# Two MLP products exchanged, two weight splits made earlier, and the last norm's squares and outputs shared out

## The chip, the cores and the metric

The kernel runs on one core of one Trainium2 chip. The time is device microseconds (us) of a whole execution. Before the change the median of three runs is 2811.76 us (2811.71 to 2813.89). Five engines appear: TensorE (PE, matmuls, with the weight loads PEld beside it), VectorE (DVE), ScalarE (ACT), GpSimd (POOL) and SyncE (SP), whose queue issues the DMA transfers in program order.

## The reference

A decoder trunk of two layers over 1024 tokens of width 1024, in float32. Layer 0 mixes tokens by a Conformer convolution, layer 1 by forgetting attention (16 heads); each then reads 256 memory tokens by cross-attention and goes through an MLP; a last RMS norm ends it.

```python
def sqrelu_mlp(h, w1, w2):                       # w1 1024 x 4096, w2 4096 x 1024
    return jnp.square(jax.nn.relu(h @ w1)) @ w2

def conformer_conv(h, ...):                      # ends with
    return u @ w_pw2 + b_pw2

for l in range(2):
    if l == 1:                                   # keys, values, gates of forgetting attention
        hk = rmsnorm(x, kv_norm_g)
        kvf = hk @ kvf_w
        ...
    h = rmsnorm(x, norm_mix_g[l])
    x = x + (conformer_conv(h, ...) if l == 0 else fox_attention(h, fox_wq, fox_wo, k, v, c))
    h = rmsnorm(x, norm_mem_g[l])
    x = x + memory_cross_attention(h, ...)
    h = rmsnorm(x, norm_ff_g[l])
    x = x + sqrelu_mlp(h, ff_w1[l], ff_w2[l])
return rmsnorm(x, final_norm_g)
```

## The kernel before

**Layout.** The residual X lies with features on partitions: 8 chunks of 128 features, each in two halves of 512 tokens, so the unit of work is a 128x512 tile. A float32 product is made of three fast passes: an operand is split into a high part (a rounding copy, on ACT, called high) and a low part (the rest, a subtraction on the DVE, called low; line 148), and high x high, low x high and high x low are added in a PSUM bank. `weights` loads a raw 512 KB weight, optionally multiplies it by a norm's gain (L256, DVE), and splits it (L151 ACT, L148 DVE).

**Stages**, by the profile: convolution layer with the matrices of the memory interleaved (to about 525 us), memory attention (to 713), MLP (713 to 1343), forgetting attention (1343 to 1966), memory attention (to 2157), MLP (2158 to 2793), last norm (to 2809). In the convolution layer and the attentions a scheduler places the instructions, by priorities and by when buffers are free. The MLP's order is written out: within `in_order` each engine takes its instructions in the order of the code.

**The MLP** (`mlp`, from L600) is two matrix products, each done by a recursion with seven products instead of eight (Strassen and Winograd). Work comes in pairs of column groups, g and g+1. A pair has seven products, in the order of `SEVEN`, each for both groups in turn, so a pair is 14 steps. A step is one product of 12 matmuls (4 chunks, 3 passes). `base[g]` is the pair's first step; g below UP = 16 is the up phase, g from 16 is the down phase, and the pair at g = 14 is the turn, with its own order. Each group sums its products in three PSUM banks:

```python
SEVEN = ("a11", "a12", "s2", "s1", "s4", "s3", "a22")
SUM = {"a11": 0, "a12": 0, "s2": 1, "s3": 1, "a22": 1, "s1": 2, "s4": 2}
```

So s2, s3 and a22 go to one bank, s1 and s4 to another, and each product adds to what the bank holds. After each product a row reads the sum as it then stands: in the up phase `rows` (L814) makes the inner activations a11, a12, a21, a22; in the down phase `add_rows` (L967, L971 in the first down pairs) adds it to X. A product may add to a bank once the row of the bank's last product has read it.

What happens at a step is put in lists, `urgent`, `before` and `after`, by `at_once`, `at` and `at_end` with the number of the step. In the up phase the inner a11 and a12 are split at given steps (`split_inner_at`: a high on ACT into a tile `uh`, a step later a low on the DVE into `ul`, both of a pool of four `t` tiles) and both parts stored to DRAM (L845); the sums s1 to s4 of the inner activations are made on POOL (L865) and stored (L826). Raw weights are loaded by `load_raw` (L639) on the same SP queue, and POOL combines them (L647). In the down phase the inner tiles are loaded again (L934, L936) and those stored whole are split there (`high_of_inner`, `low_of_inner`).

**Into forgetting attention.** `start_fox` (L1079) gives the first MLP's last steps the start of the next stage: it loads two raw weights (`wk`, the keys' first chunk, and `fox_wq`, the queries'), normalizes the first half of X chunk by chunk (h, L1095), splits it (L1096 high on ACT, L148 low on the DVE), and among the chunks, in the DVE's order after c = 2 and c = 6, multiplies the raw weights by the gain and splits them. The PE then runs the keys' product for the half, a mean of squares for the second half (L158), the queries' product, and a spread of the second half's factor (L167).

**The second linear of the convolution** (`linear` at the end of `conv_layer`) takes one raw weight per output chunk m = 0 to 7, split beside the products of the chunk before; L324 adds the result to X, once per half.

**The last norm** (from L1422): squares of X (L1006, ACT) are added up (L1014, DVE) as the MLP's last chunks come, a token mean over partitions is a matmul with a column (L158), the power -0.5 is on POOL (L207), and a matmul spreads it over partitions (L167). Eight chunks per half are multiplied by gain and factor (L1428, DVE) and stored.

## Time and profile before

| | |
|---|---|
| median of three runs | 2811.76 us |
| profiled execution, its own time | 2810.81 us |
| its span | 2809.0 us |
| mean granted PE clock | 0.993 |
| PE busy | 2725.0 us (97%) |
| DVE busy | 1991.7 us (71%) |
| ACT busy | 1275.7 us (45%) |
| POOL busy | 720.2 us (26%) |

The profile is one execution. Times count from the span's start. A timeline row gives start, length, engine, line, operation, tiles written and read, and how many instructions were put together; in brackets the idle time ahead and what ended it. A row of the waits gives the total, the number and the longest. A group's row gives, behind the bar, the busy total and the mean of one in ns. A row of windows gives the length, then the busy time (and count) of PE, PEld, DVE, ACT and POOL, the granted clock, the DMA share and GB/s.

### The profile page before, as it was taken

The page shows a single profiled execution, that of the slowest core. Times are in us where ns is not written, and L with a number is a line of the kernel's source. Part 1 is how long each engine was busy: PE and PEld are TensorE (multiplying, and loading weights), DVE is VectorE, ACT ScalarE, POOL GpSimd, SP SyncE. Part 2 cuts the span into 40 slices and gives each one's busy share as a digit, 9 for nine tenths or more (in the row PEclk, how much of TensorE's full clock was granted, in tenths as well). Part 3 has the DMA queues.
Part 4 walks back from the last instruction along what each step waited for, and adds up shares of the span by engine and source line. Part 5 has one row for each costly group of instructions (what it writes and reads, how often), then busy time and mean ns, then how long its engine had stood idle before and what let it go on. Part 6 is the DMA issues. An engine that isn't in the chain of part 4 may idle for free. (4 is left out here: it accounts for less than half of the span.)

```text
span 2809.0 us, 35852 instructions
## 1 busy us (share of the span) xinstructions
PE 2725.0 (97%) x12832; PEld 2247.6 (80%) x12832; DVE 1991.7 (71%) x3119; ACT 1275.7 (45%) x2295; POOL 720.2 (26%) x487
## 2 busy tenths in 40 slices
PE   7999999999999999999899999989999999999998
PEld 6777777888888877888688888878888788878886
DVE  5999984555776577777777777775546855677776
ACT  5112143433465563334466666663424655543332
POOL 0000000000076625784000000000000365625763
PEclk9999999999999999999899999999999999999999
DMA  6334364321265585652123222244213455565651
GB/s 220 120 120 135 110 213 124 102 91 56 80 220 181 188 303 195 214 199 91 61 87 94 89 88 77 86 143 138 96 67 105 144 183 191 203 228 194 228 203 60
DMA packets 172275, 402.26 MB, mean 143 GB/s; under 512 B 18352, under 2 KB 47408, under 8 KB 171840
## 3 DMA queue, kind: packets, MB, share of 16 engines
q1 hardware_dynamic: 171840, 399.90, 42.1%
q8 instruction: 101, 1.65, 0.2%
q14 instruction: 78, 0.64, 0.1%
q10 hardware_dynamic: 256, 0.07, 0.0%
HBM read 278.66 MB, written 117.05 MB: 141 GB/s over the span
## 5 line engine op out<-in xcount | busy, mean ns | idle before, releaser
L1070 PE MATMUL mm<-op,w 128*128 128x512 f32 x5424 | 1239.6, 390 | 20.8 <-DVE x L967 8.9
L1070 PEld LDWEIGHTS mm<-op,w 128*128 128x128 f32 x5424 | 1018.5, 188 | 238.7 <-issue 8.9
L269 PE MATMUL mm<-op,wh 128*128 128x512 f32 x1056 | 331.3, 395 | 4.7 <-DVE op L148 4.7
L148 DVE TENSOR_TENSOR w<-r,w 128x512 fp32r<-128x512 f32 x264 | 262.5, 998 | 30.2 <-ACT w L653 30.2
L653 ACT CAST w<-r 128x512 fp32r<-128x512 f32 x264 | 163.4, 623 | 259.9 <-PE mm L1070 235.2
L269 PEld LDWEIGHTS mm<-op,wh 128*128 128x128 f32 x1056 | 200.3, 190 | 50.1 <-DVE op L148 7.9
L1316 PE MATMUL mm<-op,wh 128*128 128x512 f32 x736 | 231.4, 395 | 0.0
L148 DVE TENSOR_TENSOR w<-t,w 128x512 fp32r<-128x512 f32 x180 | 176.6, 995 | 62.3 <-ACT w L653 62.0
L269 PE MATMUL mm<-op,wl 128*128 128x512 f32 x528 | 211.2, 401 | 9.4 <-DVE wl L148 6.2
L647 POOL TENSOR_TENSOR t<-r,t 128x512 f32<-128x512 f32 x104 | 174.1, 1674 | 94.4 <-DVE w L148 63.8
L207 POOL TENSOR_TENSOR r<-v,mhalf 128x4 f32<-128x4 f32 (+1 forms) x15 | 16.8, 1117 | 680.3 <-DVE v L205 680.3
L653 ACT CAST w<-t 128x512 fp32r<-128x512 f32 x180 | 111.9, 622 | 170.6 <-PE mm L1070 140.5
L865 POOL TENSOR_TENSOR x<-x,x 128x512 f32<-128x512 f32 x112 | 160.0, 1453 | 112.5 <-ACT x L878 101.6
L151 ACT CAST wh<-raw 128x1024 fp32r<-128x1024 f32 x96 | 100.6, 1049 | 190.1 <-PE mm L269 102.2
L151 ACT CAST pth<-mm 128x512 fp32r<-128x512 f32 (+1 forms) x224 | 105.9, 496 | 153.5 <-PE mm L556 80.9
L967 DVE TENSOR_TENSOR x<-mm,x 128x512 f32<-128x512 f32 x160 | 109.4, 684 | 93.1 <-PE mm L1070 75.9
L1316 PEld LDWEIGHTS mm<-op,wh 128*128 128x128 f32 x736 | 139.3, 189 | 26.9
L269 PE MATMUL mm<-op,xsh 128*128 128x512 f32 x512 | 158.0, 393 | 0.0
L1316 PE MATMUL mm<-op,wl 128*128 128x512 f32 x368 | 155.5, 423 | 2.4 <-ACT q L1336 2.4
L408 DVE SCALAR_TENSOR_TENSOR x<-d,par,x 128x512 f32<-128x512 f32 x232 | 154.5, 743 | 0.0
L647 POOL TENSOR_TENSOR t<-r,r 128x512 f32<-128x512 f32 x52 | 80.3, 1544 | 288.1 <-DMA r<-in_ff_w 239.2
L148 DVE TENSOR_TENSOR wl<-raw,wh 128x1024 fp32r<-128x1024 f32 x96 | 116.7, 1221 | 37.9 <-ACT wh L151 37.3
(187 smaller groups left out, 4569.2 us busy)
## 6 DMA issues: line engine op xcount, KB each, us to landing
r<-in_ff_w SPq DMA_DIRECT2D x128, 512.0 KB, 3.9
op<-ua SPq DMA_DIRECT2D x80, 512.0 KB, 6.8
us<-x SPq DMA_DIRECT2D x128, 256.0 KB, 2.9
op<-us SPq DMA_DIRECT2D x64, 512.0 KB, 5.3
raw<-mvo SPq DMA_DIRECT2D x32, 512.0 KB, 3.3
ua<-ul SPq DMA_DIRECT2D x64, 256.0 KB, 2.2
ua<-uh SPq DMA_DIRECT2D x60, 256.0 KB, 2.3
raw<-in_pw SPq DMA_DIRECT2D x24, 512.0 KB, 4.6
```

The lines of the kernel that those rows point to most:

```text
L148: dve.tensor_tensor(lo, src, hi.bitcast(F32), op=ALU.subtract)
L151: act.copy(hi, src)
L207: pool.tensor_tensor(r, v, mhalf[:, :nb], op=ALU.pow)
L269: pe.matmul(out_ps, x, y, start=i == 0, stop=i == len(terms) - 1)
L408: dve.scalar_tensor_tensor(out[s], d[:, j : j + n], w, y, op0=ALU.mult, op1=ALU.add)
L647: (dve if g in (2, 3, UP, UP + 1) else pool).tensor_tensor(t, raws[g, x], raws[g, y], op=ALU.subtract)
L653: act.copy(highs[n][0], raws[steps[n][:2]])
L865: eng.tensor_tensor(u[g, x], y1, y2, op=op_)
L967: dve.tensor_tensor(v, sums[key], v, op=ALU.add)
L1070: pe.matmul(sums[key], y, z, start=first and i == 0, stop=n == last_of[key] and i == len(terms) - 1, skip_group_check=True,)
L1316: pe.matmul(t, x, y, start=n == 0, stop=n == len(terms) - 1)
```

## The change

Three edits. **(1)** In `SEVEN` s3 and s4 change places, for all pairs but the turn, whose order is left, and the very last pair, which keeps the old order as `SEVEN_LAST`. The inner a12 is split two steps later (b+13 instead of b+11), the timings of the inner s3 and s4 in the down phase are exchanged, and in the first down pair s2's row comes three instead of four steps behind. **(2)** The first chunks of `wk` and `fox_wq` are multiplied and split in the convolution's second linear, ahead of chunks 3 and 5 (`split_ahead`), and the two parts of each are stored to DRAM; `start_fox` loads the parts instead of the raw weights. **(3)** At the end the last chunk's squares (3, second half) are not added to the others but get a mean of their own, added on 128x4 behind it; outputs 0 and 1 of the second half are multiplied by the gain on ACT ahead of time and by the factor on POOL, from a copy that ACT makes.

```diff
-SEVEN = ("a11", "a12", "s2", "s1", "s4", "s3", "a22")
+SEVEN = ("a11", "a12", "s2", "s1", "s3", "s4", "a22")
 SEVEN_TURN = ("a11", "a12", "s2", "s3", "s1", "a22", "s4")
+SEVEN_LAST = ("a11", "a12", "s2", "s1", "s4", "s3", "a22")
...
-    def token_mean(acc):
-
-        m = bank(ps)[:, : acc.shape[-1] // P]
-        for b in range(m.shape[-1]):
-            pe.matmul(m[:, b : b + 1], acc[:, b * P : (b + 1) * P], mean_col, start=True, stop=True)
-        return m
+    def token_mean(*accs):
+
+        nb = accs[0].shape[-1] // P
+        t = bank(ps)
+        means = [t[:, i * nb : (i + 1) * nb] for i in range(len(accs))]
+        for m, acc in zip(means, accs):
+            for b in range(nb):
+                pe.matmul(m[:, b : b + 1], acc[:, b * P : (b + 1) * P], mean_col, start=True, stop=True)
+        return means
...
+    def rms_of_sums(accs, eps, name="r"):
+
+        m, *rest = token_mean(*accs)
         nb = m.shape[-1]
         v = nrm.tile([P, 4], F32, name="v")[:, :nb]
         dve.tensor_scalar(v, m, eps, None, op0=ALU.add)
+        for x in rest:
+            dve.tensor_tensor(v, x, v, op=ALU.add)
...
-            linear(pm, lambda m: weights(a["pw2"][m]), NCH, ss, add_x)
+            def get(m):
+                if m in (3, 5):
+                    split_ahead(*(("wk", "kv"), ("fox_wq", "mix1"))[m // 4])
+                return weights(a["pw2"][m])
+
+            linear(pm, get, NCH, ss, add_x)
+
+
+    fox_first = {}
+
+    def split_ahead(name, gain):
+        parts = fox_first[name] = [dram.tile([P, NCH, P], F32, name=f"{name}{x}") for x in "hl"]
+        for d, w in zip(parts, weights(a[name][0], gain)):
+            nc.sync.dma_start(d, w.bitcast(F32))
...
-                for x in SEVEN if g + 2 != UP else SEVEN_TURN:
+                for x in {UP - 2: SEVEN_TURN, UP: SEVEN, 2 * UP - 2: SEVEN_LAST}.get(g, SEVEN):
...
-                    split_inner_at(b + (14 if last else 11) + i, g + i, "a12")
+                    split_inner_at(b + (14 if last else 13) + i, g + i, "a12")
...
-                    ("s2", (10, 12) if late else (8, 10)), ("s1", (14, 15) if late else (12, 13)), ("s4", (17, 18) if late else (16, 17)),
-                    ("s3", (20, 21) if late else (19, 20)), ("a22", (22, 23)),
+                    ("s2", (10, 12) if late else (8, 10)), ("s1", (14, 15) if late else (12, 13)), ("s3", (17, 18) if late else (16, 17)),
+                    ("s4", (20, 21) if late else (19, 20)), ("a22", (22, 23)),
...
-                    at_once(n + (4 if x in ("a12", "s2") and g < UP + 2 else 1), add_rows, n)
+                    at_once(n + (({"a12": 4, "s2": 3}.get(x, 1)) if g < UP + 2 else 1), add_rows, n)
...
-            accs, squared = {}, {}
+            accs, squared, apart = {}, {}, (3, 1) if ending is None else None
...
-                if (c, t) in squared:
+                if (c, t) in squared and (c, t) != apart:
...
-        raws = []
-
-        def load(name):
-            raws.append(raw_weights(a[name][0]))
-
-        def weight(gain):
-            ws.append(loaded(raws.pop(0), gain))
+        def load(name, x):
+            w = wp.tile([P, NCH, P], F32R, name=f"w{x}", tag=f"w{x}")
+            nc.sync.dma_start(w.bitcast(F32), fox_first[name]["hl".index(x)])
...
-            if c in (2, 6):
-                todo.append((weight, "kv" if c == 2 else "mix1"))
...
-        return [(4, partial(load, "wk")), (1, partial(load, "fox_wq"))] + [(n, partial(*f)) for n, f in zip(at, todo)]
+        loads = ((4, "wk", "h"), (4, "wk", "l"), (2, "fox_wq", "h"), (1, "fox_wq", "l"))
+        return [(n, partial(load, w, x)) for n, w, x in loads] + [(n, partial(*f)) for n, f in zip(at, todo)]
...
+        others = [] if sl.start == 0 else [X[:, c, sl] for c in (0, 1)]
+        for c, y in enumerate(others):
+            act.activation(y, y, AF.Copy, scale=col("final", c))
         rb = firsts if sl.start == 0 else spread(rms_of_sums(seconds, RMS_EPS))
+        if others:
+            rs = nrm.tile([P, HALF], F32, name="rs", tag="t", bufs=4)
+            act.copy(rs, rb)
         for c in range(NCH):
             y = X[:, c, sl]
-            dve.scalar_tensor_tensor(y, y, col("final", c), rb, op0=ALU.mult, op1=ALU.mult)
+            if c < len(others):
+                pool.tensor_tensor(y, y, rs, op=ALU.mult)
+            else:
+                dve.scalar_tensor_tensor(y, y, col("final", c), rb, op0=ALU.mult, op1=ALU.mult)
             nc.sync.dma_start(out[:, c, sl], y)
```

The PE in the first down pair of the first MLP, from s1 on: each row is half a step (6 matmuls); `mm` is the bank (one of each of the two groups), `op` the operand, `w` the weight. Before, s1 (7649 and 7669), then s4 in the same banks, then s3 (7614 and 7631):

```order
L1070 MATMUL mm_7649<-op_7403,w_7544 128x512 x6
L1070 MATMUL mm_7649<-op_7404,w_7544 128x512 x6
L1070 MATMUL mm_7669<-op_7403,w_7573 128x512 x6
L1070 MATMUL mm_7669<-op_7404,w_7573 128x512 x6
L1070 MATMUL mm_7649<-op_7505,w_7594 128x512 x6
L1070 MATMUL mm_7649<-op_7506,w_7594 128x512 x6
L1070 MATMUL mm_7669<-op_7505,w_7611 128x512 x6
L1070 MATMUL mm_7669<-op_7506,w_7611 128x512 x6
L1070 MATMUL mm_7614<-op_7362,w_7628 128x512 x6
L1070 MATMUL mm_7614<-op_7363,w_7628 128x512 x6
L1070 MATMUL mm_7631<-op_7362,w_7646 128x512 x6
L1070 MATMUL mm_7631<-op_7363,w_7646 128x512 x6
```

Now s1 (7671 and 7692), then s3 (7636 and 7653), then s4:

```order
L1091 MATMUL mm_7671<-op_7425,w_7566 128x512 x6
L1091 MATMUL mm_7671<-op_7426,w_7566 128x512 x6
L1091 MATMUL mm_7692<-op_7425,w_7595 128x512 x6
L1091 MATMUL mm_7692<-op_7426,w_7595 128x512 x6
L1091 MATMUL mm_7636<-op_7384,w_7616 128x512 x6
L1091 MATMUL mm_7636<-op_7385,w_7616 128x512 x6
L1091 MATMUL mm_7653<-op_7384,w_7633 128x512 x6
L1091 MATMUL mm_7653<-op_7385,w_7633 128x512 x6
L1091 MATMUL mm_7671<-op_7527,w_7650 128x512 x6
L1091 MATMUL mm_7671<-op_7528,w_7650 128x512 x6
L1091 MATMUL mm_7692<-op_7527,w_7668 128x512 x6
L1091 MATMUL mm_7692<-op_7528,w_7668 128x512 x6
```

s4 came two steps after s1 in the same bank and now comes four steps after it. Behind these rows stands a22 in s3's banks: two steps after s3 before, four now.

The DVE at the start of forgetting attention, before: h is a normalized chunk, `op` its low, `raw` and `wl` the weight's gain and low.

```order
L256 TENSOR_TENSOR raw<-raw,par 128x1024
L148 TENSOR_TENSOR wl<-raw,wh 128x1024
L1095 TENSOR_TENSOR h<-x_83,mm 128x512
L148 TENSOR_TENSOR op<-h,op 128x512
L967 TENSOR_TENSOR x_84<-mm,x_84 128x512
L1014 TENSOR_TENSOR sq<-sq 128x512
L1095 TENSOR_TENSOR h<-x_85,mm 128x512
...
L256 TENSOR_TENSOR raw<-raw,par 128x1024
L148 TENSOR_TENSOR wl<-raw,wh 128x1024
L1095 TENSOR_TENSOR h<-x_91,mm 128x512
L148 TENSOR_TENSOR op<-h,op 128x512 x2
```

Now, in the same place:

```order
L1116 TENSOR_TENSOR h<-x_83,mm 128x512
L149 TENSOR_TENSOR op<-h,op 128x512
L1116 TENSOR_TENSOR h<-x_85,mm 128x512
L987 TENSOR_TENSOR x_84<-mm,x_84 128x512
L1035 TENSOR_TENSOR sq<-sq 128x512
...
L1116 TENSOR_TENSOR h<-x_91,mm 128x512
L149 TENSOR_TENSOR op<-h,op 128x512
L263 TENSOR_TENSOR raw<-raw,par 128x1024
L149 TENSOR_TENSOR op<-h,op 128x512
```

Both weights' gains and lows are gone; one gain of a later weight (L263) stands ahead of the last low.

SP at the convolution's second linear, now (before, only the loads of x and `in_pw` are there):

```order
L256 DMA raw<-in_pw 128x1024
L330 DMA x<-in_xT 128x512 x2
L380 DMA wkh<-wh 128x1024
L380 DMA wkl<-wl 128x1024
L256 DMA raw<-in_pw 128x1024
L330 DMA x<-in_xT 128x512
L256 DMA raw<-in_fox_wq 128x1024
```

The stores of both parts of `wk` stand ahead of the load of a later chunk's weight; those of `fox_wq` follow in the same way.

More of the change, by code (lines that the diff above doesn't have):

```diff
@@ L198, in inverse_rms @@
         with tc.high_priority(offset=SMALL_FIRST):
-            return rms_of_sums(acc, eps)
-    def rms_of_sums(acc, eps, name="r"):
-        m = token_mean(acc)
+            return rms_of_sums([acc], eps)
+    def rms_of_sums(accs, eps, name="r"):
+        m, *rest = token_mean(*accs)
         nb = m.shape[-1]
@@ L309, in layer_norm @@
                 with tc.high_priority(offset=SMALL_FIRST):
-                    dve.tensor_scalar(nm, token_mean(acc), -1.0, None, op0=ALU.mult)
+                    dve.tensor_scalar(nm, token_mean(acc)[0], -1.0, None, op0=ALU.mult)
                 nmb = spread(nm)
@@ L595, in mem_attention @@
                 if firsts is None:
-                    firsts = rms_of_sums(sums, RMS_EPS, name="rf")
+                    firsts = rms_of_sums([sums], RMS_EPS, name="rf")
             return firsts, sums
@@ L738, in mean_second @@
             def mean_second():
-                second["r"] = rms_of_sums(seconds, RMS_EPS)
+                second["r"] = rms_of_sums([seconds], RMS_EPS)
             def spread_second():
@@ L1012, in add_square @@
             def add_square(c, t):
-                if (c, t) in squared:
+                if (c, t) in squared and (c, t) != apart:
                     dve.tensor_tensor(accs[t], accs[t], squared[c, t], op=ALU.add)
             def mean_first():
-                second["r"] = rms_of_sums(accs[0], RMS_EPS)
+                second["r"] = rms_of_sums([accs[0]], RMS_EPS)
             b = end - 14
@@ L1075, in mlp @@
                         f()
-        return second["rb"], accs[1]
+        return second["rb"], [accs[1]] + [q for k, q in squared.items() if k == apart]
     def start_fox(rb, hs, ws):
         h = {}
-        raws = []
-        def load(name):
-            raws.append(raw_weights(a[name][0]))
-        def weight(gain):
-            ws.append(loaded(raws.pop(0), gain))
+        def load(name, x):
+            w = wp.tile([P, NCH, P], F32R, name=f"w{x}", tag=f"w{x}")
+            nc.sync.dma_start(w.bitcast(F32), fox_first[name]["hl".index(x)])
+            if x == "h":
+                ws.append([w])
+            else:
+                ws[-1].append(w)
         def first(c):
@@ L1424, in trunk @@
     for sl in HALVES:
+        others = [] if sl.start == 0 else [X[:, c, sl] for c in (0, 1)]
+        for c, y in enumerate(others):
+            act.activation(y, y, AF.Copy, scale=col("final", c))
         rb = firsts if sl.start == 0 else spread(rms_of_sums(seconds, RMS_EPS))
+        if others:
+            rs = nrm.tile([P, HALF], F32, name="rs", tag="t", bufs=4)
+            act.copy(rs, rb)
         for c in range(NCH):
             y = X[:, c, sl]
-            dve.scalar_tensor_tensor(y, y, col("final", c), rb, op0=ALU.mult, op1=ALU.mult)
+            if c < len(others):
+                pool.tensor_tensor(y, y, rs, op=ALU.mult)
+            else:
+                dve.scalar_tensor_tensor(y, y, col("final", c), rb, op0=ALU.mult, op1=ALU.mult)
             nc.sync.dma_start(out[:, c, sl], y)
```

## The prediction

> **What bounds the kernel now.** I read the page's busy shares first, then what the TensorE (PE) waits for, then its timeline.
>
> ```profile
> span 2809.0 us, 35852 instructions
> PE 2725.0 (97%) x12832; PEld 2247.6 (80%) x12832; DVE 1991.7 (71%) x3119; ACT 1275.7 (45%) x2295; POOL 720.2 (26%) x487
> ```
>
> The PE is busy for 97% of the span, so the 84 us in which it stands are all that an edit without fewer products can win, together with the time in which its clock is low. The waits of the PE, summed by the line that ended them (total, number, longest):
>
> ```profile
> PE mm L1070 <- DVE x L967: 8.9, 10, 2.6
> PE mm L269 <- DVE wl L148: 6.2, 3, 4.6
> PE mm L1070 <- ACT m L955: 5.5, 2, 3.2
> PE mm L269 <- DVE op L148: 4.7, 5, 3.8
> PE mm L1070 <- DVE x L814: 3.5, 2, 3.2
> PE mm L158 <- DVE sq L1014: 2.8, 1, 2.8
> ```
>
> L1070 is the MLP's product, L967 the row that adds a sum to X in the down phase, L814 the same row in the up phase, L955 the first row of the turn. L269 holds linear products, forgetting attention's first two among them. L158 is the token mean. Each of the change's three parts aims at one or two of these rows. The PE's timeline says where they fall (start, length, matmuls, and in brackets the wait ahead):
>
> ```profile
> 793.53 239.65 PE L1070 MATMUL mm<-op,w 128*128 128x512 f32 x1056 [0.39 <-DVE x L814]
> 1036.40 27.54 PE L1070 MATMUL mm<-op,w 128*128 128x512 f32 x120 [3.22 <-ACT m L955]
> 1066.14 65.55 PE L1070 MATMUL mm<-op,w 128*128 128x512 f32 x288 [2.20 <-DVE x L967]
> 2239.49 241.28 PE L1070 MATMUL mm<-op,w 128*128 128x512 f32 x1056 [3.16 <-DVE x L814]
> 2513.18 77.94 PE L1070 MATMUL mm<-op,w 128*128 128x512 f32 x336 [2.58 <-DVE x L967]
> 2669.81 76.57 PE L1070 MATMUL mm<-op,w 128*128 128x512 f32 x336 [0.31 <-DVE x L967]
> ```
>
> Twelve matmuls are one step: 65.55 / 24 = 2.73 us. Counted in steps, the waits on L967 and L814 stand ahead of an s4 or an a22, the products that add into a bank whose last product, s1 or s3, ended one step before (the pair's other group lies between). A row must be read out of that bank first.
>
> **Part A, s3 and s4 exchanged.** Before, s1 to s4 and s3 to a22 lie two steps apart. Now s2, s3 and a22 (bank 1) and s1 and s4 (bank 2) alternate, so that both distances are four steps: a row gets 2 x 2.73 = 5.5 us more. Every wait in these rows is shorter, the longest 3.16 us. So all of 8.9 + 3.5 = 12.4 us can go. The time lost to the clock goes with them: after the 3.16 us wait 1056 matmuls took 241.28 us, after the 0.39 us wait 239.65, a loss of 1.6; after the 2.58 us wait 336 took 77.94, after the 0.31 us wait 76.57, a loss of 1.4. The bound above is thus 12.4 + 3.0 = 15.4.
>
> What may be late next is the vector engine (DVE) in the first down pair:
>
> ```profile
> 1052.00:1066.00 14.00, 11.94 (x53) 9.56 (x51) 14.00 (x15) 4.07 (x6) 12.48 (x7) 1.00 0.14 49
> 1055.66 1.77 DVE L148 TENSOR_TENSOR w<-t,w 128x512 fp32r<-128x512 f32 x1
> 1057.36 0.68 DVE L971 TENSOR_TENSOR x<-mm,m 128x512 f32<-128x512 f32 x1
> ```
>
> The first row is a window: PE 11.94, PEld 9.56, DVE 14.00, ACT 4.07 and POOL 12.48 us busy of 14.00. The DVE has no gap there; a split that takes 0.68 us elsewhere takes 1.77 beside POOL's sums. The swap takes no DVE work away. It orders the same rows so that each has at least one step between its due place and its reader; s2's row, one step earlier now and ahead of s3, has the least. Should both first down pairs keep their waits, 2.20 + 2.58 + 1.4 = 6.2 us of the 15.4 would stay and 9.2 remain. The room of 5.5 us is over twice the waits, so I am nearer to the upper bound and take off 1.5: **A = -13.9 us** (9.2 to 15.4).
>
> The a12 split moves two steps later in 12 pairs (six in each MLP). It costs no instruction; its two stores move past the raw-weight loads on SP, which is the slower rival below. Otherwise only timings of highs and lows change places.
>
> **Part B, forgetting attention's first weights.** Its start before, PE, DVE and ACT, and the PE clock in windows (the last three columns are granted clock, DMA share, GB/s):
>
> ```profile
> 1337.60 5.72 PE L1070 MATMUL mm<-op,w 128*128 128x512 f32 x24
> 1347.88 0.80 PE L269 MATMUL mm<-op,wl 128*128 128x512 f32 x1 [4.56 <-DVE wl L148]
> 1359.46 1.22 PE L269 MATMUL mm<-op,wh 128*128 128x512 f32 x2 [3.76 <-DVE op L148]
> 1371.78 1.05 PE L167 MATMUL mm<-ident,r 128*128 128x128 f32 x8
> ...
> 1344.28 1.22 DVE L256 TENSOR_TENSOR raw<-raw,par 128x1024 f32<-128x1024 f32 x1
> 1346.61 1.22 DVE L148 TENSOR_TENSOR wl<-raw,wh 128x1024 fp32r<-128x1024 f32 x1 [1.11 <-ACT wh L151]
> 1347.75 0.68 DVE L1095 TENSOR_TENSOR h<-x,mm 128x512 f32<-128x512 f32 x1
> 1354.60 1.22 DVE L256 TENSOR_TENSOR raw<-raw,par 128x1024 f32<-128x1024 f32 x1
> 1358.12 0.68 DVE L1095 TENSOR_TENSOR h<-x,mm 128x512 f32<-128x512 f32 x1
> 1358.72 1.46 DVE L148 TENSOR_TENSOR op<-h,op 128x512 fp32r<-128x512 f32 x2
> ...
> 1360.00:1370.00 10.00, 10.00 (x30) 8.14 (x29) 2.06 (x5) 0.30 (x1) 1.01 (x1) 0.53 0.09 36
> ```
>
> From 1343.32 (1337.60 + 5.72) to the spread at 1371.78 go 28.5 us for 48 matmuls and a mean. The DVE sets it: its last low ends at 1358.72 + 1.46 = 1360.18. The change takes two pieces out of the DVE's row, from L256 to the next h: 1347.75 - 1344.28 = 3.47 and 1358.12 - 1354.60 = 3.52. One gain of a later weight, 1.22, now stands ahead of the last low. So this low ends 3.47 + 3.52 - 1.22 = 5.8 us earlier, at 1354.4. Behind it stand one group of three matmuls, the mean, and the 24 matmuls of the query product, whose own weights need no DVE now. At full speed (2.73 us for 12) they take 0.7 + 1.0 + 5.5 and the spread comes at 1361.6, 10.2 us earlier. At half speed, which the 0.53 of the window shows behind the waits, they take 1.3 + 1.6 + 10.9, the spread comes at 1368.2, and 3.6 are won. The idle left is broken into pieces: a low every 1.2 us (L1095 and L148, 0.6 each) against 0.7 us of matmuls. Nothing in the trace shows which clock such a pattern gets, so I take near the middle: **B = -7.2 us** (3.6 to 10.2).
>
> The weights' loads are no wait: the products need them at about 1344, and the first two loads stand four steps (10.9 us) ahead of the MLP's end; a load of 512 KB landed in 3.8 us in the last row of the next fence.
>
> The splitting itself moves to the second linear of the convolution:
>
> ```profile
> 458.90 0.75 DVE L324 SCALAR_TENSOR_TENSOR x<-mm,par,x 128x512 f32<-128x512 f32 x1 [3.31 <-PE mm L269]
> 464.33 0.75 DVE L324 SCALAR_TENSOR_TENSOR x<-mm,par,x 128x512 f32<-128x512 f32 x1 [3.13 <-PE mm L269]
> raw<-in_pw SPq DMA_DIRECT2D x4, 512.0 KB, 3.8
> ```
>
> A chunk comes every 2 x 5.43 = 10.9 us, and the DVE is idle for 3 us ahead of each L324. An extra gain, high and low are 1.22 + 1.11 + 1.22 by the rows at 1344.28 and 1346.61 (1.11 is the DVE's wait for ACT's high), 3.5 us, done before the slot's next user. Their four stores of 512 KB go out on SP; the slot must be clear of them before the next split, and no such store is in this trace: by loads of that size 3.8 us. I calculate split done 461, stored 465, next split done 467, needed 470. **So 0**, with 3 us of loss as the bound below.
>
> **Part C, the last norm.** The end before, PE, POOL and DVE, then an ACT copy and a POOL product of 128x512 tiles elsewhere, and the end's stores:
>
> ```profile
> 2795.64 1.28 PE L158 MATMUL mm<-mean_col,sq 128*128 128x1 f32 x8 [2.79 <-DVE sq L1014]
> 2797.20 1.01 POOL L207 TENSOR_TENSOR r<-v,mhalf 128x4 f32<-128x4 f32 x1 [12.27 <-DVE v L205]
> 2800.38 5.36 DVE L1428 SCALAR_TENSOR_TENSOR x<-x,par,mm 128x512 f32<-128x512 f32 x8 [3.26 <-PE mm L167]
> L653 ACT CAST w<-r 128x512 fp32r<-128x512 f32 x264 | 163.4, 623 | 259.9 <-PE mm L1070 235.2
> L1187 POOL TENSOR_TENSOR o<-o,ri 128x512 f32<-128x512 f32 x14 | 18.2, 1297 | 213.4 <-DMA ri<-rd 213.4
> out_y<-x SPq DMA_DIRECT2D x16, 256.0 KB, 2.1
> GB/s 11 0 0 0 0 23 0 0 0 0 0 0 203 158 299 393 31 347 373 3 62 390 271 201 161 0 0 0 0 0 254 384 370 393 376 381 387 348 0 0
> ```
>
> With the last square's add gone from its path (0.6 at the row's pace) and no scaling of another chunk between, the mean starts about 1.2 earlier; the small add behind it costs 0.2. The spread is there 1.0 earlier, at 2799.4. But chunks 0 and 1 now go over ACT's copy (0.62 by L653's row) and two POOL products of 1.30: ready at 2801.4 and 2802.7 instead of 2801.1 and 2801.7. SP issues in order, so six chunks that the DVE has ready stand behind them. The last row shows the transfers: slices of 0.725 us, from 2801.8 to 2807.5 at about 380 GB/s, so the eight stores fill the transfer time. Seven of 262 kB from 2802.7 take 4.8 us after the issue: the end comes between 0.5 earlier and 2 later, and I take **C = +1.0**.
>
> Sum: -13.9 - 7.2 + 0 + 1.0 = -20.1. The profiled execution took 2810.81 us (1.8 around its span of 2809.0), so it comes to 2790.7. The median of the runs before, 2811.76, lies 0.95 higher: **2791.7 us**.
>
> By the Trainium skill's "TensorE: Matmul & The Clock Gate" (Part 1) the clock halves only after an idle window of about 3.4 us. By that rule B is worth its full 10.2, and the 2.58 us wait of A should have cost no clock. The trace disagrees there (1.4 us lost behind it), though the 3.22 us wait at the turn was followed by 120 matmuls in 27.54 us, which is full speed.
>
> **The rivals.** *Full clock at the start of forgetting attention*: no idle piece there is over 1.3 us now, and the turn's row speaks for it, the loss behind 2.58 against it. B is 10.2: 2811.76 - 13.9 - 10.2 + 1.0 = 2788.7.
>
> *The waits only move*: the full DVE window speaks for it, the 5.5 us of room against. A 9.2, B 3.6, C +2: 2811.76 - 10.8 = 2801.0.
>
> *The split is not hidden*, so part B doesn't do what it says: both splits stand on the PE's path for 3.5 each behind the stores, 2791.7 + 7 = 2798.7. For it: the store has no row; against it the 10.9 us of each chunk.
>
> *Slower, by SP's queue.* In the up phase a store that waits for its data holds the raw loads behind it, and now the a12 stores stand there two steps later:
>
> ```profile
> SPq L845 <- DVE ul L148: 52.5, 20, 4.8
> 2240.00:2380.00 140.00, 140.00 (x612) 115.71 (x612) 82.53 (x102) 78.45 (x134) 86.13 (x59) 0.99 0.52 183
> ```
>
> These SP waits are of 2260 to 2440 us, 52.5 / 20 = 2.6 us each. If each of the 12 moved pairs passed one on to the PE, through raw loads or through the four `t` buffers that uh and ul share, it would be 12 x 2.6 = 31.5 us: 2823. From 1.7 us a pair it takes all that the rest wins. Against it: with the same waits of SP, the PE is busy for 140.00 of 140 us.
>
> **How the numbers follow.** Chances: the sum 0.52 (its terms' bounds give 2785.7 to 2804), full clock 0.14, waits moved 0.18, split not hidden 0.08, slower 0.08. The range 2785 to 2804 leaves out the slower case and the ends. A measurement of this kernel tells 0.2%, 5.6 us, from no change. Only the slower case, and a little of the two small-gain cases, lies above 2806.1: faster 0.86, same 0.08, slower 0.06.
>
> **What would show it.** A: no wait on L967's or L814's successor above 0.5 us in the timeline of either MLP but in the last pair, and 1056 matmuls in under 240 us in both. B: the wait of 4.56 gone and the spread about 21 us after the last MLP product instead of 28.5; the second linear's chunks still 10.9 us apart. C: SP's last stores issued behind POOL's two products. The forecast is wrong if waits on DVE of 2 us stand in the first down pairs, if SP's or `t`'s waits come up in the PE's list, or if the convolution's end moves.

## The result, and the profile after

The changed kernel takes 2793.39 us (median of six runs, 2791.90 to 2797.75) against 2812.82 us before (six runs beside it, 2809.71 to 2815.79): a ratio of 0.993 with a 95% interval of 0.9918 to 0.9943. The forecast was 2791.7. The profiled execution's span is 2790.1 us, 18.9 less than before, and splits by stages as follows (starts and ends of products and spreads from the PE's timeline, us):

| stage | before | after | forecast of the difference | measured |
|---|---|---|---|---|
| start to first product of the first MLP | 714.8 | 714.9 | 0 | +0.1 |
| first MLP, first to last product | 628.5 | 626.0 | A: -13.9 for both MLPs | -2.5 |
| last product to spread, forgetting attention | 28.5 | 18.2 | B: -7.2 | -10.3 |
| spread to first product of the second MLP | 786.2 | 789.0 | 0 | +2.8 |
| second MLP, first to last product | 634.9 | 626.2 | with the first MLP | -8.7 |
| last product to the span's end | 16.15 | 15.86 | C: +1.0 | -0.3 |

What the PE waits for after the change (total, number, longest), the rows that answer to those of before:

```profile
PE mm L276 <- ACT mem L471: 8.8, 2, 8.4
PE mm L1091 <- ACT m L975: 8.7, 2, 4.4
PE mm L1386 <- DVE mn L1392: 6.7, 11, 2.0
...
PE mm L276 <- DVE op L149: 3.3, 6, 2.3
...
PE mm L276 <- DVE wl L149: 1.5, 2, 1.0
...
PE mm L162 <- ACT sq L1027: 0.4, 1, 0.4
```

Every line moved, by 1 to 30: L1091 is the MLP's product (L1070 before), L975 the turn's first row (L955), L276 the linear product (L269). The rows for L967 and L814 are gone altogether: no product waits for a row of s1, s3, s4 or a22 any more. In their place the turn's row has grown, from 5.5 us in two waits to 8.7. The PE's timeline shows what is left of both MLPs' down phases:

```profile
1036.91 293.67 PE L1091 MATMUL mm<-op,w 128*128 128x512 f32 x1284 [4.30 <-ACT m L975]
...
2470.11 293.85 PE L1091 MATMUL mm<-op,w 128*128 128x512 f32 x1284 [4.36 <-ACT m L975]
```

From the turn on, 1284 matmuls run without a gap. They take 0.2287 and 0.2289 us each, against 0.2269 (239.65 / 1056) at full clock before: 2.3 and 2.5 us are lost to the clock behind the two waits. A window around the end of the first wait shows it, after and then before the change (the third column from the end is the granted clock):

```profile
1035.09:1041.92 6.83, 5.01 (x12) 3.94 (x13) 6.80 (x12) 5.67 (x10) 0.00 (x0) 0.50 0.64 199
1035.09:1041.92 6.83, 5.52 (x24) 4.56 (x25) 6.80 (x12) 6.64 (x11) 0.00 (x0) 1.00 0.66 228
```

The start of forgetting attention, PE and DVE:

```profile
1335.13 5.72 PE L1091 MATMUL mm<-op,w 128*128 128x512 f32 x24
1346.40 1.22 PE L276 MATMUL mm<-op,wh 128*128 128x512 f32 x2 [2.28 <-DVE op L149]
1350.41 1.05 PE L276 MATMUL mm<-op,wh 128*128 128x512 f32 x2
1354.48 0.63 PE L276 MATMUL mm<-op,wh 128*128 128x512 f32 x2
1359.04 1.05 PE L171 MATMUL mm<-ident,r 128*128 128x128 f32 x8
...
1349.86 1.22 DVE L263 TENSOR_TENSOR raw<-raw,par 128x1024 f32<-128x1024 f32 x1
1350.99 0.69 DVE L149 TENSOR_TENSOR op<-h,op 128x512 fp32r<-128x512 f32 x1
```

The first product starts with no wait. One wait of 2.28 us is left, for a low; behind it two matmuls take 1.05 us (half speed), later 0.63 (full speed). The last low ends at 1351.68, and the spread comes at 1359.04, 18.2 us after the last MLP product (1340.85).

Later in the same stage 2.8 us are lost. The first attention scores wait for a minimum that needs the gates, which come back from DRAM (DVE, PE, and the window behind; before, the same rows showed waits of 1.46 and 0.58):

```profile
1399.07 0.29 DVE L1392 CUSTOM_DVE_ANT_0 x<-mm,cj 128x128 f32<-128x128 f32 x1 [2.80 <-DMA cj<-cd]
1399.43 0.44 PE L1386 MATMUL mm<-kl,qs 128*128 128x384 f32 x1 [2.01 <-DVE mn L1392]
1399.50:1409.50 10.00, 10.00 (x49) 8.25 (x50) 8.32 (x28) 6.58 (x19) 0.00 (x0) 0.83 0.16 53
```

The PE's wait is 1.4 us longer, and the granted clock of 0.83 in the next 10 us costs another 1.7 (0.17 of 10).

The end, PE, DVE, POOL:

```profile
2775.75 1.05 PE L162 MATMUL mm<-mean_col,sq 128*128 128x1 f32 x8 [0.41 <-ACT sq L1027]
2778.42 1.30 PE L171 MATMUL mm<-ident,r 128*128 128x128 f32 x8 [1.62 <-POOL r L214]
2780.43 4.04 DVE L1458 SCALAR_TENSOR_TENSOR x<-x,par,mm 128x512 f32<-128x512 f32 x6 [3.22 <-ACT rs L1452]
2780.47 2.48 POOL L1456 TENSOR_TENSOR x<-x,rs 128x512 f32<-128x512 f32 x2 [2.11 <-ACT rs L1452]
```

The last product ends at 2774.24. The spread is done 5.5 us later (2778.42 + 1.30), against 7.5 before (2798.26 + 2.08 - 2792.85): 2.0 us won. But the DVE does not start on it at 2779.72. It waits 0.7 us for ACT's copy of the spread (rs), although it doesn't read the copy.

### The profile page after: what moved, and what is told of

The parts are those of the page before. It is cut to its first block, busy times and chain, and to the rows that moved or that the text cites. A ratio compares the mean times of both kernels' runs of the same rounds, so it can differ in the third digit from the quotient of the medians.

```text
span 2790.1 us, 35867 instructions
## 1 busy us (share of the span) xinstructions
PE 2721.3 (98%) x12840; PEld 2247.6 (81%) x12840; DVE 2008.3 (72%) x3117; ACT 1277.5 (46%) x2298; POOL 729.7 (26%) x489
## 5 line engine op out<-in xcount | busy, mean ns | idle before, releaser
L1091 PE MATMUL mm<-op,w 128*128 128x512 f32 x5424 | 1237.8, 390 | 11.4 <-ACT m L975 8.7
L1091 PEld LDWEIGHTS mm<-op,w 128*128 128x128 f32 x5424 | 1020.7, 188 | 225.4 <-ACT m L975 9.5
L276 PE MATMUL mm<-op,wh 128*128 128x512 f32 x1056 | 329.3, 393 | 3.3 <-DVE op L149 3.3
L149 DVE TENSOR_TENSOR w<-r,w 128x512 fp32r<-128x512 f32 x264 | 274.3, 1042 | 32.8 <-ACT w L673 18.5
L276 PEld LDWEIGHTS mm<-op,wh 128*128 128x128 f32 x1056 | 198.6, 189 | 48.5 <-DVE op L149 7.2
L149 DVE TENSOR_TENSOR w<-t,w 128x512 fp32r<-128x512 f32 x180 | 193.4, 1089 | 32.8 <-ACT w L673 32.6
L276 PE MATMUL mm<-op,wl 128*128 128x512 f32 x528 | 209.6, 398 | 5.0 <-ACT op L152 3.5
L276 PE MATMUL mm<-op,xsh 128*128 128x512 f32 x512 | 157.8, 393 | 0.0
```

Of the source, the lines that this page charges most:

```text
L149: dve.tensor_tensor(lo, src, hi.bitcast(F32), op=ALU.subtract)
L276: pe.matmul(out_ps, x, y, start=i == 0, stop=i == len(terms) - 1)
L1091: pe.matmul(sums[key], y, z, start=first and i == 0, stop=n == last_of[key] and i == len(terms) - 1, skip_group_check=True,)
```

## The experiments

Eleven kernels. Time per stage in the profiled execution of each, "turn" the sum of both waits at the turn (the row L975 of the changed kernel), "ratio" against runs of the kernel before on the same chip:

| kernel | first MLP starts | first MLP | B's start | to second MLP | second MLP | turn | end | median, us | ratio (95%) |
|---|---|---|---|---|---|---|---|---|---|
| before | 714.8 | 628.5 | 28.5 | 786.2 | 634.9 | 5.5 | 16.15 | 2812.82 | 1 |
| changed | 714.9 | 626.0 | 18.2 | 789.0 | 626.2 | 8.7 | 15.86 | 2793.39 | 0.993 (0.9918 to 0.9943) |
| e1, A alone | 713.1 | 626.8 | 28.3 | 788.3 | 625.3 | 8.7 | 15.97 | 2799.54 | 0.9954 (0.9939 to 0.9968) |
| e2, B alone | 716.3 | 628.4 | 17.8 | 790.8 | 632.8 | 6.0 | 16.77 | 2806.0 | 0.9972 (0.996 to 0.9984) |
| e3, C alone | 711.3 | 629.2 | 27.0 | 791.0 | 633.6 | 4.5 | 15.85 | 2812.73 | 1.0007 (0.9997 to 1.0017) |
| e4 | 715.2 | 625.1 | 17.8 | 788.7 | 626.4 | 9.2 | 14.56 | 2789.82 | 0.9919 (0.9904 to 0.9933) |
| e5 | 717.7 | 626.4 | 17.8 | 789.8 | 626.8 | 8.6 | 16.36 | 2790.61 | 0.9923 (0.9891 to 0.9955) |
| e6 | 718.0 | 625.5 | 17.8 | 788.2 | 626.3 | 8.9 | 16.10 | 2793.88 | 0.9944 (0.9927 to 0.9962) |
| e7 | 714.3 | 628.3 | 17.8 | 788.4 | 630.3 | 15.5 | 16.18 | 2799.5 | 0.9963 (0.9948 to 0.9977) |
| e8 | 715.8 | 627.0 | 17.9 | 787.6 | 627.3 | 9.4 | 14.23 | 2792.62 | 0.9933 (0.9913 to 0.9953) |
| e9 | 719.4 | 621.2 | 18.2 | 788.3 | 624.5 | 4.5 | 14.94 | 2784.86 | 0.9896 (0.9881 to 0.9911) |
| e10 | 715.6 | 621.7 | 17.8 | 788.2 | 623.3 | 4.4 | 14.51 | 2785.04 | 0.990 (0.9882 to 0.9918) |
| e11 | 721.2 | 627.2 | 18.2 | 791.2 | 627.1 | 9.5 | 15.18 | 2793.69 | 0.9938 (0.9926 to 0.995) |

The start of the first MLP scatters by 10 us and the stretch to the second MLP by 5, so the theories are judged by the stage they speak of, not by the span.

### e1 to e3: each part alone

**e1**, part A on the kernel before:

```diff
-SEVEN = ("a11", "a12", "s2", "s1", "s4", "s3", "a22")
+SEVEN = ("a11", "a12", "s2", "s1", "s3", "s4", "a22")
...
-                    split_inner_at(b + (14 if last else 11) + i, g + i, "a12")
+                    split_inner_at(b + (14 if last else 13) + i, g + i, "a12")
...
-                    at_once(n + (4 if x in ("a12", "s2") and g < UP + 2 else 1), add_rows, n)
+                    at_once(n + (({"a12": 4, "s2": 3}.get(x, 1)) if g < UP + 2 else 1), add_rows, n)
```

> Part A alone on the kernel before. If the parts add up, as the two traces suggest, the MLPs take from first to last product 626.0 and 626.2 us, as in the changed kernel (before: 628.5 and 634.9), forgetting attention's start stays at 28.5 us and the end at 16.1, and the span is 2809.0 - 11.2 = 2797.8. The turn's wait for ACT's first copies (before 3.2 and 2.3 us) is then about 4.3 in both MLPs. Rival: the turn's longer wait comes from part B's or C's extra work; then it stays at 3.2 and 2.3 here, the MLPs take about 625 and 623, and the span is near 2794.7.

Measured: span 2797.7, the MLPs 626.8 and 625.3 (11.3 less together), and the turn's waits are 8.7 us, as with all parts:

```profile
PE mm L1078 <- ACT m L962: 8.7, 2, 4.6
PE mm L276 <- DVE wl L149: 6.2, 3, 4.6
PE mm L1374 <- DVE mn L1380: 5.7, 11, 1.1
```

The rows for L967 and L814 are missing here too. The longer turn belongs to part A.

**e2**, part B on the kernel before:

```diff
+                if m in (3, 5):
+                    split_ahead(*(("wk", "kv"), ("fox_wq", "mix1"))[m // 4])
...
+        loads = ((4, "wk", "h"), (4, "wk", "l"), (2, "fox_wq", "h"), (1, "fox_wq", "l"))
```

> Part B alone. From the first MLP's last product to the spread 18.2 us instead of 28.5, MLPs as before. From the spread to the second MLP's first product the changed kernel took 789.0 us against 786.2 before. If that give-back belongs to part B (other instruction order in forgetting attention), it is 789.0 here too and the span is 2809.0 - 7.5 = 2801.5. Rival: it is the landing time of one broadcast load, which differs from one execution to the next; then it is nearer 786.2 and the span near 2798.7. In both cases the convolution's second linear stays where it was (first MLP product at 714.8, within 0.3).

Measured: B's start 17.8 us, the stretch behind it 790.8, span 2802.9. By itself this would speak for the give-back belonging to B. But without B the stretch is 786.2, 788.3 and 791.0 (before, e1, e3), with B 787.6 to 791.2: the two groups overlap over nearly their whole width, and the longest wait for the minimum in e3, without B, is 1.8 us. So no run shows that the give-back belongs to B: the stretch differs from one execution to the next, and the kernel before happened to have the shortest. That the landing of one load decides it, as the rival said, is not shown.

The first MLP product came at 716.3 us and not at 714.8 within 0.3, as expected in both cases, and the median fell by only 7.0 us (2813.01 before on the same chip; by the ratio's interval, 4.5 to 11.3), where B's start alone won 10.7. The second linear of the convolution takes as long as forecast, first and last result of before and after (DVE):

```profile
445.98 0.75 DVE L324 SCALAR_TENSOR_TENSOR x<-mm,par,x 128x512 f32<-128x512 f32 x1 [4.39 <-PE mm L269]
524.58 0.75 DVE L324 SCALAR_TENSOR_TENSOR x<-mm,par,x 128x512 f32<-128x512 f32 x1
```

```profile
445.97 0.75 DVE L331 SCALAR_TENSOR_TENSOR x<-mm,par,x 128x512 f32<-128x512 f32 x1 [4.35 <-PE mm L276]
524.81 0.75 DVE L331 SCALAR_TENSOR_TENSOR x<-mm,par,x 128x512 f32<-128x512 f32 x1
```

78.60 us without and 78.84 with both splits: 0.24 us for 3.5 us of work on two engines, twice, and four stores. But ahead of it part B has a cost. Up to about 385 us the PE's order is the same in all thirteen kernels; from there (the PE's 1552nd matmul) to the second linear's first result it takes 59.3 to 59.8 us in the three profiled executions without B, 59.9 and 60.0 in two with it (the changed kernel and e8), and 62.0 to 65.4 in the other eight. With B the scheduler puts more matmuls of the memory's matrices ahead of a token mean of the convolution. In these eight the PE waits 1.2 to 3.0 us for that mean (0.5 to 1.3 in the other five), and in these eight alone its clock is at half there, for 3.4 or 6.8 us. How the new order brings this about isn't shown. The mean before, then in e4, with the window behind it:

```profile
387.13 1.05 PE L158 MATMUL mm<-mean_col,acc 128*128 128x1 f32 x8 [0.61 <-DVE acc L354]
```

```profile
386.80 1.05 PE L162 MATMUL mm<-mean_col,acc 128*128 128x1 f32 x8 [1.48 <-DVE acc L361]
388.59:392.00 3.41, 3.41 (x13) 2.96 (x12) 2.16 (x4) 1.31 (x3) 0.00 (x0) 0.50 0.16 20
```

**e3**, part C on the kernel before:

```diff
+            accs, squared, apart = {}, {}, (3, 1) if ending is None else None
...
+        others = [] if sl.start == 0 else [X[:, c, sl] for c in (0, 1)]
```

> Part C alone. From the last product to the end of the span 15.9 us instead of 16.15, so the span is 2808.7 and the ratio cannot be told from 1. The factor is spread 2 us earlier after the last product (5.5 instead of 7.5 us), and the vector engine's first output waits 0.7 us for ACT's copy, the first store for POOL. Rival: the whole 2 us arrive, span 2807.0.

Measured: end 15.85 instead of 16.15, ratio 1.0007 (0.9997 to 1.0017). Part C as a whole is worth 0.3 us by this pair of executions, which the time can't tell from nothing (without part C, e1 ends in 15.97 and e2 in 16.77).

### e4 and e11: where part C's two microseconds go

**e4**, the changed kernel without outputs on ACT and POOL; the last squares' mean stays apart:

```diff
-        others = [] if sl.start == 0 else [X[:, c, sl] for c in (0, 1)]
+        others = []
```

> The changed kernel, but the eight outputs of the last half all on the vector engine, as before; only the last squares' mean stays apart. If the outputs on ACT and POOL hold the stores back, the end after the last product is 14.2 us instead of 15.9, and the span 2790.1 - 1.7 = 2788.4. Rival: the transfers bound the end whatever comes first, 15.9 again and the span 2790.1.

Measured: end 14.56, span 2787.8, ratio 0.9919. The DVE now starts as soon as the spread is done (2777.42 + 1.64 = 2779.06):

```profile
2777.42 1.64 PE L171 MATMUL mm<-ident,r 128*128 128x128 f32 x8 [1.62 <-POOL r L214]
2779.10 5.35 DVE L1458 SCALAR_TENSOR_TENSOR x<-x,par,mm 128x512 f32<-128x512 f32 x8 [2.89 <-PE mm L171]
```

So the mean apart wins 1.6 us, and sharing the outputs gives 1.3 of it back. These are single executions; over all of them the ends are 15.97 to 16.77 without part C (three), 15.85 to 16.36 with all of it and the old order of stores (five) and 14.23 to 14.94 with the mean apart alone (four), so both differences stand in sign.

**e11**, the changed kernel with the store of chunk 1 behind those of chunks 2 to 7:

```diff
-            nc.sync.dma_start(out[:, c, sl], y)
+            if c >= len(others):
+                nc.sync.dma_start(out[:, c, sl], y)
+        for c, y in enumerate(others):
+            nc.sync.dma_start(out[:, c, sl], y)
```

> The changed kernel with the store of chunk 1 of the last half behind those of chunks 2 to 7 on SP (chunk 0's store still comes first, its place is the scheduler's). Same instructions otherwise. If the loss of part C is SP's in-order queue, where six finished chunks stand behind POOL's second product (1.24 us), the end after the last product falls by about that, from 15.9 to between 14.7 and 15.0. If the loss is the vector engine's wait of 0.7 us for ACT's copy, or the transfers themselves, it stays at 15.9 to 16.4, the spread of the four kernels measured so far with these outputs.

Measured: end 15.18, just above the theory's 14.7 to 15.0 and below the 15.85 to 16.36 of the five kernels with the old order of stores. SP's in-order queue is thus about half of the loss: 0.7 of 1.3 us against the changed kernel (15.86 - 15.18), 0.9 of 1.5 against the means of the groups (16.07 and 14.56). It is one execution, and the slowest of its kernel's seven. The DVE still waits for ACT's copy here, and chunk 0's store still comes first; between these two the rest is not told apart.

### e5 to e8: why the turn's wait grew

**e5**, the a12 split one step earlier, so that its stores stand ahead of the raw loads again:

```diff
-                    split_inner_at(b + (14 if last else 13) + i, g + i, "a12")
+                    split_inner_at(b + (14 if last else 12) + i, g + i, "a12")
```

> The changed kernel with the inner a12 split one step earlier (b+12 instead of b+13), so that in every pair of the up phase both its stores stand ahead of the next raw loads on SP, not behind them. Theory: the turn's wait grew from 5.5 to 8.7 us (both MLPs together) because these stores moved behind the loads; then it falls by about half of the growth, to 7.1, and with the clock the span by 2 us. Rival: the wait grew because the PE arrives earlier at a chain on SP, DVE and ACT that did not get faster; then it stays at 8.7 within 0.5 and the span at 2790 within 1.5.

Measured: turn 8.6 us, as the rival said. The stores' new place isn't the cause. (The span of 2794.8 is outside what either theory gave; the kernel's median is 2790.61.)

**e6 and e7**, the raw loads of the first down pair (second halves) one step earlier and one step later:

```diff
-                        at(b - 6 + i + 2 * late, load_raw, g + i, 1)
+                        at(b - 6 + i + 1 * late, load_raw, g + i, 1)
```

```diff
-                        at(b - 6 + i + 2 * late, load_raw, g + i, 1)
+                        at(b - 6 + i + 3 * late, load_raw, g + i, 1)
```

> The changed kernel with the second halves of the raw weights of the first down pair issued one step earlier; on SP only one load moves, that of the second group, ahead of two loads of inner tiles. Theory: the turn's wait is the landing of that load, issued at 1021.2 although its tile is free from 1014.9; issued about 2.3 us earlier the wait falls by about that in each MLP, 8.7 to about 4.5, the clock loss behind it with it, and the span falls by 4 to 6 us. Rival: DVE and ACT have the work of the turn to do anyway, or the load of the first group decides; then the wait stays within 1 us of 8.7.

> The changed kernel with the same two raw loads one step (2.7 us) later. If their landing sets the turn's wait, it grows by about 2.7 us in each MLP, from 8.7 to about 14, and the span by 5 to 8 us. If DVE's and ACT's own work sets it, it grows by less than 2 us in all.

Measured: earlier 8.9 us, later 15.5. The DVE's first combination of these weights, in the changed kernel and in e7:

```profile
1026.27 0.69 DVE L667 TENSOR_TENSOR t<-r,r 128x512 f32<-128x512 f32 x1 [3.27 <-DMA r<-in_ff_w]
```

```profile
1028.61 0.69 DVE L667 TENSOR_TENSOR t<-r,r 128x512 f32<-128x512 f32 x1 [5.73 <-DMA r<-in_ff_w]
```

The landing of a raw load does set the wait: later loads lengthen it, by even more than the step, as they now stand behind the two loads of the inner s1 too. But in e6 only the load of the second group found an earlier place on SP, and the DVE waits for the first group's. My theory had the wrong load of the two. The traces agree on this throughout: in all thirteen, in both MLPs, the PE goes on 10.6 us after that combination starts (1026.27 to 1036.91 in the changed kernel, 1028.61 to 1039.24 in e7), and the DVE has no gap in between. So the wait at the turn ends when the first group's load has landed and this work is done, however early the PE arrives.

**e8**, e4 and e6 together:

> The changed kernel with both: all eight last outputs on the vector engine, and the raw load of the turn one step earlier. The gains are in different places and add: end 14.6 us instead of 15.9 (measured alone), turn as in the kernel with the early load. Span 2787.8 - 4 to 6 = 2782 to 2784 if the load sets the turn's wait, 2787.8 if it doesn't.

Measured: end 14.23, turn 9.4, span 2789.8. As by e6, the second edit is worth nothing.

### e9 and e10: bytes ahead of the raw load

In the changed kernel's windows the DMA share (last column but one) is about 1 for the 30 us before the turn, and its rate (last) is among the highest of the program:

```profile
985.00:995.00 10.00, 10.00 (x46) 8.29 (x45) 8.12 (x9) 7.02 (x13) 5.87 (x5) 1.00 0.40 112
995.00:1005.00 10.00, 10.00 (x45) 8.27 (x45) 3.21 (x5) 5.60 (x11) 9.68 (x7) 1.00 0.99 377
1005.00:1015.00 10.00, 10.00 (x46) 8.26 (x44) 6.68 (x11) 3.13 (x6) 0.00 (x0) 1.00 1.04 409
1015.00:1025.00 10.00, 10.00 (x46) 8.28 (x45) 4.41 (x6) 6.08 (x10) 0.00 (x0) 1.00 1.03 389
```

The raw load was issued at 1018.05 behind two loads of the inner s3, 512 KB each, and its data were there at 1026.2. At the turn the inner tiles are loaded in the order of `SEVEN_TURN`, where s3 stands ahead of s1, but the first down pair uses s3 after s1. The same two loads stood ahead of the raw load before the change, so this is no consequence of the swap, which even moved s3's first use two steps nearer. **e9** is e8 with s3 loaded behind both raw loads; **e10** is e4 with s3 so placed, the raw loads at their old steps:

```diff
-                    at(lb + 2 * k + 2, load_inner, f, x)
+                    at(lb + (11 if not f and x == "s3" else 2 * k + 2), load_inner, f, x)
```

> The changed kernel with all last outputs on the vector engine (end 14.6 us) and, at each MLP's turn, both second halves of the raw weights issued one step earlier and the inner s3 (two loads of 512 KB, first needed six steps later) loaded behind them. Theory: the turn's wait is the landing of the first group's raw load, and that load queues behind bytes: the transfers run at 380 to 410 GB/s for the 30 us before it. 1.05 MB less ahead of it is 2.6 us at 400 GB/s, and a place about 1.3 us earlier in SP's queue; so the wait falls from about 4.5 to 1 to 2 us in each MLP, part of the clock loss behind it (1.5 us each) goes too, and the span is 2787.8 - 6 to 8 = 2780 to 2782. Rival: the DMA engines share bandwidth among all open transfers, and whatever is taken from ahead comes back beside it, or the next load or ACT's and DVE's own work of the turn takes the place at once; then the wait stays above 3.5 us in each and the span above 2785.

> As the one before, but the raw loads keep their steps; only the inner s3 is loaded behind them. The theory of bytes gives the larger part of the gain, 2.6 us in each MLP, wait about 2 us, span 2782 to 2784. If instead the place in the queue decides (the step at which the raw load is issued), the wait stays above 3.5 us.

Measured: turn 4.5 and 4.4 us, MLPs 621.2 and 624.5, 621.7 and 623.3. In e10 (PE's waits, then the DVE's first combination):

```profile
PE mm L1091 <- ACT m L975: 4.4, 2, 2.3
...
1024.72 0.69 DVE L667 TENSOR_TENSOR t<-r,r 128x512 f32<-128x512 f32 x1 [0.27 <-DMA r<-in_ff_w]
```

The DVE's wait for the raw load fell from 2.84 us (e4) to 0.27, and the PE's from 9.2 to 4.4 for both turns, 2.0 and 2.3 us, as expected for e10; e9's 1.9 and 2.6 are at and above the upper end of its 1 to 2. What stands ahead of the load counts. Counted from the MLP's first product, it is issued 1.4 and 0.8 us sooner than in e4 and then lands 0.8 and 1.8 us faster, so SP's issuing and the bytes both have a part. A step earlier adds nothing in e9, where little was left to win: the rest of the PE's wait is the 10.6 us of the DVE's and ACT's own work. e9's span of 2786.5 lies above the 2780 to 2782 expected, and above the 2785 that was to speak for the rival, but its first MLP began 4.5 us later than the changed kernel's; e10's 2781.2 is just below its 2782 to 2784.

e9 and e10 beat both kernels: 0.9896 and 0.990 against 0.993, e9's interval wholly below the changed kernel's. Against e4, which shares their last norm, the intervals overlap, and the gain is seen in the MLPs: 1245.0 us together in e10 against 1251.5. No run tries the later load on the kernel before.

## Why the prediction was right, point by point

The sum was -20.1 us, the spans differ by -18.9 and the medians by -19.4. The terms were off by more than that, in both directions: A was 2.7 us too large and 2.8 us of give-back in forgetting attention were not in the sum, B was 3.1 too small and C 1.3. That it came within 1.2 us is in part luck.

**A: -13.9 forecast, -11.2 measured (e1 alone: -11.3).** The mechanism is as described: all 12.4 us of waits on L967 and L814 are gone, in both first down pairs too, so the 1.5 us taken off for them weren't needed. Two steps failed. One is "where a stall goes": I looked for the next late one in the first down pair's full DVE window and passed over the turn's row, which I had quoted: its 5.5 us were counted as unchanged, and they grew by 3.2. There the PE waits for a chain that begins with transfers running at the DMA engines' full rate. In the second MLP the PE reached the turn 5.1 us earlier, but the load landed, and the wait ended, only 3.0 us earlier (counted from the MLP's first product: 325.1 before, 322.1 after). In the first MLP both came 0.4 later; what held that load back on SP is open, beyond its not being the a12 stores (e5).

The other is the clock: 3.0 us were to come back with the waits. The PE's busy time at a clock of 0.50 was 3.41 + 3.17 us before, all in the second MLP behind the waits of 3.16 and 2.58; now it is 5.01 us in the first and 5.41 in the second, behind the turn. At half of each, the clock costs 1.9 us more than before and not 3.0 less. What made up for it is something the sum had left out. By the starts of the matmuls, a wait costs some 0.3 us beyond the idle time that its row shows, and there are twelve waits fewer: an estimate of 3.3 us. Waits -9.4, clock +1.9 and these -3.3 come to -10.8 of the 11.2.

**B: -7.2 forecast, -10.3 measured.** The DVE's part of the sum held: last low 10.8 us after the last product, 11.1 forecast. The mis-sized term is the clock behind it. I took the middle between full and half speed for the last 27 matmuls and the mean; they ran at full speed, 1359.04 - 1351.68 = 7.4 us against 7.2 at full and 13.8 at half. So the rival of the full clock came true, by another way than I gave it: the clock did fall behind the 2.28 us wait, and was back at 1352.5, 0.8 us behind the last low. The wait also had a cover I hadn't seen: at half speed the PE no longer outran the DVE, so the following lows cost no wait. And the trace before did show which clock a low every 1.2 us gets, further on in the same stage, where two matmuls take 0.73 us beside the 1.05 at half speed:

```profile
1353.53 0.73 PE L269 MATMUL mm<-op,wh 128*128 128x512 f32 x2 [0.23 <-DVE op L148]
1354.73 0.73 PE L269 MATMUL mm<-op,wh 128*128 128x512 f32 x2 [0.23 <-DVE op L148]
```

**The splitting in the convolution: 0 forecast.** In the second linear itself it was 0.24 us. The step that failed is that nothing else there would change: the scheduler's order changed ahead of it, and from 385 us to the second linear the ten executions with B take 62.5 us in the mean against 59.6 in the three without, 2.9 us more (59.9 to 65.4 against 59.3 to 59.8, see e2). The profiled execution of the changed kernel is one of the two that show only 0.3 of it; it is also the fastest of its six.

**C: +1.0 forecast, -0.3 measured.** Queue and in-order stores behave as forecast (e11), and POOL's two products took 1.24 us each for the 1.30 used. The spread came 2.0 us earlier instead of 1.0: the mean started at 1.5 us after the last product where it had been 2.8, and the spread's matmuls took 1.30 us instead of 2.08. The second goes with the clock: half speed began 2.0 us ahead of the spread before and 0.9 us behind its start now. Not foreseen was the DVE's wait for ACT's copy.

**The rivals.** The slower one had the right queue, SP, and the wrong transfers, place and price: 3.2 us at the turns, not 31 in the up phase. "The waits only move" took about a quarter of A. The range of 2785 to 2804 held the time near its middle.

## What to carry to other kernels

When a group of waits is to be removed, look for the next place downstream where the engine already waits a little for transfers at full rate: an earlier arrival there is a longer wait. At such a place, order loads by first use. Handing work to idle engines was no gain here, where the consumer is one in-order queue, and a second reader of a result delayed the first. Ask also what a scheduler will reorder elsewhere when it is given more to place.

## What the runs showed of the hardware

- **The clock changes on a grid of 3.41 us.** In all thirteen traces the half-speed stretches start a whole number of steps of 3.413 us apart and last a whole number of them, but for the one that runs into the end. The changed kernel:

```profile
1031.68:1035.09 3.41, 0.93 (x5) 0.43 (x3) 3.37 (x7) 0.67 (x2) 0.00 (x0) 1.00 0.51 204
1041.92:1045.33 3.41, 3.41 (x17) 2.79 (x16) 3.41 (x6) 1.88 (x3) 0.00 (x0) 1.00 1.04 392
1345.70:1352.52 6.82, 6.12 (x14) 4.35 (x15) 6.46 (x12) 2.17 (x4) 0.00 (x0) 0.50 0.07 22
1400.32:1403.73 3.41, 3.41 (x11) 2.49 (x10) 3.34 (x9) 1.42 (x5) 0.00 (x0) 0.50 0.09 14
```

  With the stretch from 1035.09 shown above, the starts lie 91 and 107 steps apart (310.61 and 365.23 us). A wait's length alone does not tell what it costs: half speed came with waits of 2.01 and 2.28 us here, and none with the 3.22 us at the turn of the kernel before. That fits a clock that is decided at the grid's steps, so that the place of a wait counts too; the rule itself the runs don't show. The Trainium skill's "TensorE: Matmul & The Clock Gate" (Part 1) has the clock halve after an idle window of about 3.4 us and come back after as long a busy one. The length agrees. The fall doesn't, as a bound on one idle stretch. The return agrees from 1400.32 to 1403.73, but not always: before the change the half speed that came with the wait of 3.76 us lasted three steps, from 1359.24 to 1369.48, with matmuls all the while (a token mean among them).
- **The DVE waited for ACT's read of the same PSUM bank.** The DVE's first output starts 0.04 us after ACT's copy of the spread ends (2780.39), 0.7 us after the spread. The Trainium skill's "PSUM — Partial Sum Buffer" (PSUM bank collisions raise a hardware error) says that the compiler's scheduler puts a dependency between any two instructions of different engines on the same bank, reads against reads included. The trace agrees.
- **The DMA engines moved 409 GB/s over 10 us** (1005 to 1015) at a share of 1.04, with loads and stores mixed. The Trainium skill's "DMA: Bandwidth & Descriptors" (Specifications) gives 435 GB/s as the fabric's ceiling and about 358 as the memory's share per core; the trace lies above the second.
